# Two-layer trunk on one core: weight units made four ahead in five buffers, the norm's steps placed anew

## The chip, the core and the metric

One core of a Trainium2 chip runs the whole program, in one launch. Its engines have in-order instruction streams of their own: TensorE multiplies matrices (PE in the profile; its loads of stationary operands are PEld), VectorE (DVE) and ScalarE (ACT) work on tiles in SBUF and PSUM, SyncE (SP) issues the weight loads. PSUM has eight banks; TensorE writes nowhere else. The metric is the device time of one execution in microseconds (us).

## The reference

Two layers on 256 positions of width 1024, all in float32:

```
h += 0.5*SwiGLU(RMSNorm(h))                 (ffn1, width 2816)
u  = RMSNorm(h); one input projection of u feeds
     sparse attention (top-k keys), causal pooling, Mamba-2 SSD, three gates
h += W_out( sum_b sigmoid(gate_b) * Lift_b(branch_b) )
h += 0.5*SwiGLU(RMSNorm(h))                 (ffn2)
h += sigmoid(RMSNorm(h) W_g) * (p[i] W_p)   (ple)
```

and a last RMSNorm. RMSNorm divides a position by the root of the mean of its squares. The SSD branch has an RMSNorm of its own, over its 1024 channels, ahead of its lift. The gain of a norm is applied to the channels before a matmul; the factor r of a position can be multiplied in behind the matmul, since it belongs to a column of the result. The kernel uses that nearly everywhere.

## The kernel before

**Units.** All weights are cut into units of 128 x 1024 float32 (512 KB), 229 a layer, numbered here in the order in which they are used: 0 to 65 for ffn1, 66 to 69 for the narrow part of the input projection (704 columns each), 70 to 128 for the rest of the projection, the key-value matrices and the pooling, 129 to 144 for the lift, 145 to 152 for the output, then ffn2 and, from 219, ple; the second layer starts with unit 229. A unit is loaded by SP into a buffer `raw` (L135), rounded by ScalarE to `whi` (L136), and VectorE writes the remainder `wlo = raw - whi` (L137). A product then takes three matmuls (`mm3`, L159 to L161): uh x whi, ul x whi, uh x wlo, where uh and ul are the same two halves of the activations. A full unit feeds 24 matmuls of 128 x 128 by 256 columns.

**Ahead.** `unit()` makes the unit that is asked for and the next AHEAD = 3; `raw`, `whi` and `wlo` have four buffers each. So the cast and the remainder of unit n wait until TensorE has read unit n-4, and its load until VectorE has read the raw of n-4.

**Order.** Each engine's order of work is written by a scheduler that runs when the program is built: it goes by the code's order, by priorities, and by its own clock model of when operands will be there. Only TensorE's matmuls and transposes keep the program's order among those that pass `self.mm` and `self.transpose`. At run time the order of an engine is fixed; an instruction at its head that waits holds all behind it.

**The norm (`rnorm`).** The squares are added up in `acc` while h is written. Then: two matmuls by a column of ones (L106) sum over the channels; VectorE makes 1/sqrt by three Newton steps of two columns (`rsqrt`, L188 to L202); it writes two diagonal matrices dh and dl (L246, L247); two matmuls with a matrix of ones (`onesr`, L106; called the broadcast matmuls here) spread them to `pr`, in one of four `aux` banks; ScalarE copies `pr` to `r` (L255). `later()` runs the next piece of it, so it stands between the matmuls of the next stage. The results of that stage wait in four `mm` banks until r is there.

**Mix.** Its narrow projection (66 to 69) goes to two `aux` banks, then units 70 to 73 give the indexer's queries; VectorE takes their first bank pair by L437, writes u = h * gain * r by L446, and ScalarE and VectorE split u into uh and ul (L175, L176). From unit 74 on the matmuls read this u. The SSD's decay rates go through DRAM: written at L813, fetched back in broadcast by SP into three buffers `ab` (L820, L823), scanned on VectorE (L879).

**Lift.** For each of eight channel groups c, one unit multiplies attention and pooling into bank p1, another the SSD into p2. VectorE frees p1 by L593, and p2 by L597 and L598: t2 = (g3 + 1) * rs, t2 = t2 * p2, where rs is the r of the SSD's norm, whose matmuls stand among the lift's own.

Of the kernel before, what the change touches and what calls it, by code (L numbers as in the profile page):

```python
# [9 lines left out]
F = mybir.dt.float32  # L10
FR = mybir.dt.float32r
I32 = mybir.dt.int32
AF = mybir.ActivationFunctionType
OP = mybir.AluOpType
AX = mybir.AxisListType

P = 128
D = 1024
S = 256
# [4 lines left out]
EPS = 1e-6  # L24
NEG = -3.0e38
UNIT = 1024
# [38 lines left out]
class Builder:  # L65
# [43 lines left out]
        self.tc.keep_in_program_order(self.nc.tensor.transpose(*args))  # L109


    AHEAD = 3

    def unit(self, *key):
        self.used.append(key)
# [3 lines left out]
        assert self.order[i] == key  # L119
        for j in range(len(self.made), min(i + self.AHEAD, len(self.order) - 1) + 1):  # L120
            self.made.append(self.load(*self.order[j]))
        return self.made[i]

    def parts(self):
        raw = self.wp.tile([P, UNIT], F, tag="raw", name=self.name("raw"), bufs=4)
        hi = self.wp.tile([P, UNIT], FR, tag="whi", name=self.name("whi"), bufs=4)
        if self.gap is None:
            self.gap = self.wp.tile([P, LINE // 4], F, name="gap")
        lo = self.wp.tile([P, UNIT], FR, tag="wlo", name=self.name("wlo"), bufs=4)
        return raw, hi, lo  # L130

    def load(self, layer, u, n):
# [86 lines left out]
    def rnorm(self, late=False, gap=1):  # L219

        nc = self.nc
        r = self.t([P, S], tag="rs_r", bufs=3)
        v = self.t([P, 2], tag="rs_v", bufs=2)
        rc = self.t([P, 8], tag="rs_y", bufs=2)
        acc = None if late else self.acc

        def steps():
            nonlocal acc  # L230
            if late:
                for c in range(KD):
                    self.square(c, self.h[:, c])
                    if c % 4 == 3:
                        yield
                acc = self.acc
            ps = self.bank("aux")
            for h in range(2):
                self.mm(ps[:, h:h + 1], acc[:, h * P:(h + 1) * P], self.ones[:, :1],
                                 start=True, stop=True)  # L240
            nc.vector.tensor_scalar(v, ps[:, :2], 1.0 / D, EPS, op0=OP.mult, op1=OP.add)
            self.rsqrt(rc, v, 2)
            dh, dl = (self.t([P, 2, P], FR, tag="t1") for _ in range(2))
            for h in range(2):
                x = rc[:, h:h + 1]
                nc.vector.tensor_scalar(dh[:, h], self.ident, x, None, op0=OP.mult)  # L246
                nc.vector.scalar_tensor_tensor(dl[:, h], self.ident, x, dh[:, h].bitcast(F),  # L247
                                               op0=OP.mult, op1=OP.subtract)
            for _ in range(gap):
                yield  # L250
            pr = self.bank("aux")
            for i, d in enumerate((dh, dl)):
                self.mm(pr[:, :S], self.onesr, d.rearrange("p a b -> p (a b)"),
                                 start=(i == 0), stop=(i == 1))
            nc.scalar.copy(r, pr[:, :S])  # L255

        self.todo = steps()
        return rc, r

# [131 lines left out]

    def mix(self, layer, nxt):
        nc = self.nc
        rc, r = self.rnorm()
        rb = r[:, None, :].to_broadcast([P, 2, S])
        u0 = self.uh, self.ul

# [3 lines left out]
        big1 = self.a([P, KF, S], F, "gh")  # L401
        big2 = self.a([P, KF, S], F, "gl")
        ga = big1[:, :16].rearrange("p (a b) s -> p a b s", a=2)
        bc, cn = big1[:, 16:20], big1[:, 20:22]
        g3, zs = big2[:, :8], big2[:, 8:16]
        cb = big2[:, 16:19].rearrange("p a (b c) -> p a b c", b=2)
        idx = big2[:, 19:21]
        sm = self.a([P, 2, 96], F, "sm")[:, :, :88]
        ki2 = self.a([P, 2, 2, 64], F, "ki2")
        ss = self.t([P, 4], tag="ss", bufs=1)  # L410
        pb = []
        for h in range(2):
            ts = slice(h * P, (h + 1) * P)
            ps = self.bank("aux")
            for k in range(KD):
                w = wu[k // 2]
                s = slice((k % 2) * BF, (k % 2) * BF + 344)
                self.mm3(ps[:, :344], (u0[0][:, k, ts], u0[1][:, k, ts]),
                         (w[0][:, s], w[1][:, s]), k == 0, k == KD - 1)
            self.later()  # L420
            pb.append(ps)
        for h, ps in enumerate(pb):
            nc.scalar.mul(cn[:, h], ps[:, :256], rc[:, h:h + 1])
# [9 lines left out]
        for i in range(0, 4, 2):  # L433
            ps = self.in_pair(layer, T_QI + i, u0)
            self.later()
            t = self.t([P, 2, S])
# [7 lines left out]
        for k in range(KD):  # L444
            t = self.t([P, S], tag="t1")
            nc.vector.scalar_tensor_tensor(t, self.h[:, k], self.col(layer, "mix_norm", k), r,  # L446
                                           op0=OP.mult, op1=OP.mult)
# [4 lines left out]
        xs = self.a([P, 8, S], F, "uh", 2)  # L452
        q = [self.a([P, 4, S], FR, "a4", 7) for _ in range(2)]
# [77 lines left out]
        res = {}  # L531
# [25 lines left out]
            yield from self.attention(mb, q, kt, vt, ya)  # L557

        def states():
            res["ssd"] = yield from self.ssd(layer, sm, xs, bc, cb, zs)  # L560

        def pools():
            wpl = self.unit(layer, U_POOL, 512)
# [7 lines left out]
        with self.tc.issue_after(self.last.ins):  # L571
            self.weave((states(), 56), (attend(), 34), (pools(), 24), (gate, 43), apart=(0, 1))
        ysh, ysl, rs = res["ssd"]

        mh = self.a([P, 8, S], FR, "uh", 2)
        ml = self.a([P, 8, S], FR, "ul", 2)
        for c in range(8):
            p1, p2 = self.bank(), self.bank()
            w = self.unit(layer, U_LIFT + 2 * c, 1024)
            for b, y in enumerate((ya, yp)):  # L580
                for k in range(4):
                    s = slice((b * 4 + k) * P, (b * 4 + k + 1) * P)
                    self.mm3(p1[:, b * S:(b + 1) * S], (w[0][:, s], w[1][:, s]),
                             (y[:, 0, k], y[:, 1, k]), k == 0, k == 3)
            self.later()
            w = self.unit(layer, U_LIFT + 2 * c + 1, 1024)
            for k in range(8):
                s = slice(k * P, (k + 1) * P)
                self.mm3(p2[:, :S], (w[0][:, s], w[1][:, s]),
                         (ysh[k // 4][:, k % 4], ysl[k // 4][:, k % 4]), k == 0, k == 7)  # L590
            self.later()
            t = self.t([P, 2, S])
            nc.vector.scalar_tensor_tensor(t, ga[:, :, c], 1.0,  # L593
                                           p1.rearrange("p (a b) -> p a b", a=2),
                                           op0=OP.add, op1=OP.mult)
            t2 = self.t([P, S], tag="t1")
            nc.vector.scalar_tensor_tensor(t2, g3[:, c], 1.0, rs, op0=OP.add, op1=OP.mult)  # L597
            nc.vector.tensor_tensor(t2, t2, p2[:, :S], op=OP.mult)  # L598
            nc.vector.tensor_tensor(t[:, 0], t[:, 0], t[:, 1], op=OP.add)
            nc.vector.tensor_tensor(t2, t[:, 0], t2, op=OP.add)  # L600
            self.split(mh[:, c], ml[:, c], t2)
        self.new_u()
        for cs in ((0, 1), *((c,) for c in range(2, 8))):
            ps = [self.bank()[:, :S] for _ in cs]
# [167 lines left out]
        yield lambda: out(1)  # L772
        done(1)

    def ssd(self, layer, sm, xs, bc, cb, zs):
        nc = self.nc


        x = self.t([P, 2, 16], tag="dt_x", bufs=1)
# [16 lines left out]
        for k in (15, 13, 11, 9, 7, 5, 3):  # L796
# [5 lines left out]
                                       op0=OP.mult, op1=OP.mult)  # L802
        yield

        ps = self.bank("aux")
# [7 lines left out]
        nc.sync.dma_start(dram, rows)  # L813
        yield

        def fetch(g, h, q):
            x = self.t([P, 4, P], tag="ab", bufs=3)
            if q < 2:
                k = h * 16 + g * 8 + q * 4
                nc.sync.dma_start(x, dram[None, k:k + 4, :].to_broadcast([P, 4, P]))  # L820
            else:
                for i in range(2):
                    nc.sync.dma_start(x[i * 64:(i + 1) * 64],  # L823
                                      dram[None, 16 + g * 8 + i:16 + g * 8 + 8:2, :]
                                      .to_broadcast([64, 4, P]))
            return x

        wanted = [(g, h, q) for g in range(2) for h, q in ((0, 0), (0, 1), (1, 0), (1, 1), (1, 2))]
        rates = {}

        def rate(*key):
            i = wanted.index(key)
            for k in wanted[i:i + 3]:
                if k not in rates:
                    rates[k] = fetch(*k)
            return rates[key]


        for i, (a, b) in enumerate(((0, 0), (1, 1), (0, 1))):
            ps = self.bank("aux")  # L840
# [3 lines left out]
            v = ps[:, :S].rearrange("p (a b) -> p a b", a=2)  # L844
# [8 lines left out]
        for h in range(2):  # L853
            for g in range(2):
                ps = self.bank("aux")
# [12 lines left out]
        ps = self.bank("aux")  # L868
# [3 lines left out]
        for g in range(2):  # L872
            gs = slice(g * 4, (g + 1) * 4)
            for h in range(2):
                ms = self.a([P, 2, 4, P], F, "ct")
                for q in range(2):
# [9 lines left out]
                                            op=OP.mult)  # L886
                    yield
                ps = self.bank("aux")

                def near():  # L890
                    for j in range(8):
# [15 lines left out]
                                    op=OP.mult)  # L907
            po = self.bank("aux")
            e1 = self.t([P, 4, P])
            x = rate(g, 1, 2)  # L910
# [5 lines left out]
            for j in range(4):  # L916
                a = x0[:, 2 * j:2 * j + 2].rearrange("p a b -> p (a b)")
# [10 lines left out]
            for i in range(4):  # L928
                k = g * 4 + i
# [2 lines left out]
                self.split_scaled(ysh[g][:, i], ysl[g][:, i], y[:, k],  # L932
                                  self.col(layer, "ssd_norm", k))
                yield
        _, rs = self.rnorm()
        return ysh, ysl, rs

    def pool_group(self, layer, g, ps, wpl, yp):
# [242 lines left out]
```

## Time and profile before

| | |
|---|---|
| three runs | 1340.24, 1342.32, 1345.29 us; median 1342.32 |
| the profiled execution | 1341.97 us, of which 1340.1 are the span of its records |
| busy in that span | TensorE 98%, VectorE 78%, ScalarE 55% |
| DMA | 248.24 MB, mean 185 GB/s |
| TensorE's granted clock | 9 of 10 or more in all 40 slices |

How to read it: the span is cut into what each engine did and what it waited for. TensorE's matmuls are pipelined: one of 256 columns takes about 0.28 us from its start to its end, but in a steady row the next one starts 0.113 us later. So what TensorE loses at one place is read from the starts: the distance between two of them, less that pace. The waits that the profile names are a little shorter, since they count only from the end of the matmul before.

### The profile page before, as it was taken

What the parts mean: (1) busy time and instruction counts of PE and PEld (TensorE: products, weight loads), DVE (VectorE), ACT (ScalarE), POOL (GpSimd) and SP (SyncE); (2) the same over time, 40 slices, a digit from 0 to 9 for tenths busy, and PEclk for the clock granted to TensorE, in tenths of its full rate; (3) what the DMA queues carried; (4) which work ended last, traced back from release to release, by engine and by line L of the source; (5) the groups of instructions that cost most, each with busy time, mean ns of one, the idle gap of its engine ahead of it and who ended that gap; (6) DMA issues with size and microseconds to landing.
All of it is one profiled execution on the core that took longest, in us unless ns stands there. A gap on an engine that the chain in (4) does not pass through costs nothing.

```text
span 1340.1 us, 28299 instructions
## 1 busy us (share of the span) xinstructions
PE 1312.0 (98%) x11502; PEld 1297.7 (97%) x11502; DVE 1040.5 (78%) x1971; ACT 740.4 (55%) x1209; POOL 5.3 (0%) x17
## 2 busy tenths in 40 slices
PE   7999999999999999999999999999999999999997
PEld 7999999999999999999999999999999999999997
DVE  7877668987989777766887766779789888777666
ACT  5554446656864555544654454556477645555454
POOL 0000000000000000000000000000000000000000
PEclk9999999999999999999999999999999999999999
DMA  7666656576646666666556666546655556666661
GB/s 257 191 192 198 192 158 201 158 208 192 189 128 199 191 200 191 194 197 191 187 162 200 192 191 197 188 135 196 195 190 163 175 180 204 190 191 195 197 190 63
DMA packets 72385, 248.24 MB, mean 185 GB/s; under 512 B 7936, under 2 KB 10304, under 8 KB 72256
## 3 DMA queue, kind: packets, MB, share of 16 engines
q1 hardware_dynamic: 71392, 245.17, 59.5%
q8 instruction: 90, 1.47, 0.5%
q10 hardware_dynamic: 864, 1.28, 0.3%
q14 instruction: 39, 0.32, 0.1%
HBM read 245.33 MB, written 1.08 MB: 184 GB/s over the span
## 4 chain that ended last, share of the span: by engine, by line
PE 94%; DVE 3%; ACT 1%; issue 0%; DMA 0%; SPq 0%; DVEq 0%; ACTq 0%
PE mm L159 29%; PE mm L160 29%; PE mm L161 29%; PE aux L106 3%; PE aux L159 1%; PE aux L160 1%; PE aux L161 1%; DVE wlo L137 1%; PE aux L109 1%; ACT whi L136 0%; DMA h<-in_x_dram 0%; DVE t L446 0%; DVE t L993 0%; ACT t L213 0%; DVE ct L879 0%
## 5 line engine op out<-in xcount | busy, mean ns | idle before, releaser
L136 ACT CAST whi<-raw 128x1024 fp32r<-128x1024 f32 (+1 forms) x457 | 475.0, 1045 | 491.1 <-issue 245.2
L159 PE MATMUL mm<-uh,whi 128*128 128x256 f32 x2560 | 708.3, 278 | 12.6 <-ACT whi L153 6.7
L137 DVE TENSOR_TENSOR wlo<-raw,whi 128x1024 fp32r<-128x1024 f32 (+1 forms) x457 | 553.5, 1214 | 212.8 <-ACT whi L136 209.6
L160 PE MATMUL mm<-ul,whi 128*128 128x256 f32 x2560 | 709.0, 278 | 0.9 <-DVE ul L176 0.9
L161 PE MATMUL mm<-uh,wlo 128*128 128x256 f32 x2560 | 707.5, 278 | 2.0 <-DVE wlo L137 1.9
L159 PEld LDWEIGHTS mm<-uh,whi 128*128 128x128 f32 x2560 | 480.5, 188 | 15.9 <-ACT whi L153 6.7
L161 PEld LDWEIGHTS mm<-uh,wlo 128*128 128x128 f32 x2560 | 481.3, 188 | 3.2 <-DVE wlo L137 2.6
L160 PEld LDWEIGHTS mm<-ul,whi 128*128 128x128 f32 x2560 | 482.1, 188 | 2.3 <-DVE ul L176 1.3
L161 PE MATMUL mm<-gh,wlo 128*128 128x256 f32 x704 | 194.1, 276 | 0.0
L160 PE MATMUL mm<-gl,whi 128*128 128x256 f32 x704 | 194.1, 276 | 0.0
L159 PE MATMUL mm<-gh,whi 128*128 128x256 f32 x704 | 193.7, 276 | 0.0
L160 PEld LDWEIGHTS mm<-gl,whi 128*128 128x128 f32 x704 | 132.2, 188 | 0.0
L161 PEld LDWEIGHTS mm<-gh,wlo 128*128 128x128 f32 x704 | 132.2, 188 | 0.0
L159 PEld LDWEIGHTS mm<-gh,whi 128*128 128x128 f32 x704 | 131.9, 188 | 0.0
L159 PE MATMUL mm<-a,whi 128*128 128x256 f32 x256 | 69.8, 278 | 3.2 <-DVE t L593 1.3
L160 PE MATMUL mm<-a,whi 128*128 128x256 f32 x256 | 70.4, 277 | 0.0
L161 PE MATMUL mm<-a,wlo 128*128 128x256 f32 x256 | 70.3, 276 | 0.0
L159 PEld LDWEIGHTS mm<-a,whi 128*128 128x128 f32 x256 | 47.4, 188 | 4.0 <-issue 3.9
L160 PEld LDWEIGHTS mm<-a,whi 128*128 128x128 f32 x256 | 48.1, 188 | 0.0
L161 PEld LDWEIGHTS mm<-a,wlo 128*128 128x128 f32 x256 | 48.1, 188 | 0.0
L352 DVE TENSOR_TENSOR t<-mm,rs_r 128x256 f32<-128x256 f32 x88 | 37.3, 423 | 11.2 <-ACT rs_r L255 1.4
L357 DVE SCALAR_TENSOR_TENSOR t<-t,t 128x256 f32<-128x256 f32 x88 | 37.4, 425 | 3.1
(211 smaller groups left out, 1096.8 us busy)
## 6 DMA issues: line engine op xcount, KB each, us to landing
raw<-in_w_dram SPq DMA_DIRECT2D x447, 512.0 KB, 3.6
ab<-rates SPq DMA_DIRECT2D x16, 256.0 KB, 4.1
raw<-in_w_dram SPq DMA_DIRECT2D x8, 352.0 KB, 3.0
raw<-in_w_dram SPq DMA_DIRECT2D x4, 256.0 KB, 4.7
ab<-rates SPq DMA_DIRECT2D x8, 128.0 KB, 3.3
h<-in_x_dram SPq DMA_DIRECT2D x2, 256.0 KB, 4.2
h<-in_x_dram SPq DMA_DIRECT2D x1, 512.0 KB, 6.1
t<-in_p_dram ACTq DMA_DIRECT2D x2, 256.0 KB, 5.0
```

What stands on the lines that cost most here:

```text
L106: self.tc.keep_in_program_order(self.nc.tensor.matmul(*args, **kw))
L109: self.tc.keep_in_program_order(self.nc.tensor.transpose(*args))
L136: nc.scalar.copy(hi[:, :n], raw[:, :n])
L137: nc.vector.tensor_tensor(lo[:, :n], raw[:, :n], hi[:, :n].bitcast(F), op=OP.subtract)
L159: mm(ps, a[0], b[0], start=start, stop=False)
L160: mm(ps, a[0], b[1], start=False, stop=False)
L161: mm(ps, a[1], b[0], start=False, stop=stop)
L352: nc.vector.tensor_tensor(t, p1[0], r, op=OP.mult)
L357: nc.vector.scalar_tensor_tensor(g, th, 1.0, t, op0=OP.add, op1=OP.mult)
```

## The change

`AHEAD` is 4, and `whi` and `wlo` have five buffers; `raw` still has four. The rates are fetched into six rows of the tile `big1` that the gates will use later (`room`) and no longer into `ab`, and the small tile ki2 comes from the pool t1. In the lift, p2 is multiplied by the gate (g3 + 1) first, without rs, so both banks of a group can be freed before rs is known; groups that have no rs yet stand in the list `waiting`, and the product by rs is made for all of them once the norm has run through. In `rnorm`, the short steps and the copy to r stand under `high_priority(offset=160)`. The norms of mix and of the SSD have `gap=2` for 1, and in the narrow projection `later()` is called after every fourth block and not once at its end. No instruction is added or taken away; each engine has as many as before.

```diff
-    AHEAD = 3
+    AHEAD = 4
...
-        hi = self.wp.tile([P, UNIT], FR, tag="whi", name=self.name("whi"), bufs=4)
+        hi = self.wp.tile([P, UNIT], FR, tag="whi", name=self.name("whi"), bufs=5)
...
-        lo = self.wp.tile([P, UNIT], FR, tag="wlo", name=self.name("wlo"), bufs=4)
+        lo = self.wp.tile([P, UNIT], FR, tag="wlo", name=self.name("wlo"), bufs=5)
...
-        r = self.t([P, S], tag="rs_r", bufs=3)
+        r = self.t([P, S], tag="rs_r", bufs=2)
...
+            with self.tc.high_priority(offset=160):
+                ps = self.bank("aux")
...
+            with self.tc.high_priority(offset=160):
+                nc.scalar.copy(r, pr[:, :S])
...
-        rc, r = self.rnorm()
+        rc, r = self.rnorm(gap=2)
...
-        ki2 = self.a([P, 2, 2, 64], F, "ki2")
+        ki2 = self.t([P, 2, 2, 64], tag="t1")
...
-            self.later()
+                if k % 4 == 3:
+                    self.later()
...
+        waiting = []
...
-            nc.vector.scalar_tensor_tensor(t2, g3[:, c], 1.0, rs, op0=OP.add, op1=OP.mult)
-            nc.vector.tensor_tensor(t2, t2, p2[:, :S], op=OP.mult)
+            nc.vector.scalar_tensor_tensor(t2, g3[:, c], 1.0, p2[:, :S], op0=OP.add, op1=OP.mult)
             nc.vector.tensor_tensor(t[:, 0], t[:, 0], t[:, 1], op=OP.add)
-            nc.vector.tensor_tensor(t2, t[:, 0], t2, op=OP.add)
-            self.split(mh[:, c], ml[:, c], t2)
+            waiting.append((c, t, t2))
+            if self.todo is None:
+                for c1, t, t2 in waiting:
+                    nc.vector.tensor_tensor(t2, t2, rs, op=OP.mult)
+                    nc.vector.tensor_tensor(t2, t[:, 0], t2, op=OP.add)
+                    self.split(mh[:, c1], ml[:, c1], t2)
+                waiting = []
...
-            x = self.t([P, 4, P], tag="ab", bufs=3)
+            i = wanted.index((g, h, q)) % 3 * 2
+            x = room[:, i:i + 2].rearrange("p a (b c) -> p (a b) c", b=2)
...
-        _, rs = self.rnorm()
+        _, rs = self.rnorm(gap=2)
```

How the order moves, at the places that the prediction speaks of. First VectorE at the start of mix in layer 0, before; wlo_2628 and wlo_2663 are the remainders of units 74 and 75, rk is the norm of the indexer's keys, and L437 is the first instruction that reads r (rs_r):

```order
L137 TENSOR_TENSOR wlo_2628<-raw_2626,whi_2627 128x1024
L191 TENSOR_SCALAR rk_2768<-rs_t_2770 128x4
L195 TENSOR_TENSOR rs_t_2770<-rk_2768,rs_h_2769 128x4
L196 TENSOR_TENSOR rs_t_2770<-rs_t_2770,rk_2768 128x4
L137 TENSOR_TENSOR wlo_2663<-raw_2661,whi_2662 128x1024
L202 SCALAR_TENSOR_TENSOR rk_2768<-rs_t_2770,rk_2768 128x4
L437 TENSOR_TENSOR t_386_2656<-mm_2595,rs_r_2471 128x512
L446 SCALAR_TENSOR_TENSOR t_397_2727<-h,cc_93,rs_r_2471 128x256
```

The same place now; wlo_2634, wlo_2669 and wlo_2699 are units 75, 76 and 77, and L440 is the old L437:

```order
L137 TENSOR_TENSOR wlo_2634<-raw_2632,whi_2633 128x1024
L191 TENSOR_SCALAR rk_2774<-rs_t_2776 128x4
L137 TENSOR_TENSOR wlo_2669<-raw_2667,whi_2668 128x1024
L195 TENSOR_TENSOR rs_t_2776<-rk_2774,rs_h_2775 128x4
L137 TENSOR_TENSOR wlo_2699<-raw_2697,whi_2698 128x1024
L196 TENSOR_TENSOR rs_t_2776<-rs_t_2776,rk_2774 128x4
L440 TENSOR_TENSOR t_389_2662<-mm_2601,rs_r_2477 128x512
L449 SCALAR_TENSOR_TENSOR t_400_2733<-h,cc_93,rs_r_2477 128x256
```

The last remainder ahead of the first use of r was unit 75's and is now unit 77's. On ScalarE it is the same: before, the casts of units 74 and 75 stood ahead of the copy to r,

```order
L136 CAST whi_2627<-raw_2626 128x1024
L136 CAST whi_2662<-raw_2661 128x1024
L255 COPY rs_r_2471<-aux_2577 128x256
L136 CAST whi_2692<-raw_2691 128x1024
L175 CAST a_377_2593<-t_386_2656 128x512
```

and now those of 75, 76 and 77 do, with 78 right behind it:

```order
L136 CAST whi_2633<-raw_2632 128x1024
L136 CAST whi_2668<-raw_2667 128x1024
L136 CAST whi_2698<-raw_2697 128x1024
L257 COPY rs_r_2477<-aux_2571 128x256
L136 CAST whi_2795<-raw_2794 128x1024
L175 CAST a_380_2599<-t_389_2662 128x512
```

TensorE around the second broadcast matmul of that norm, now; whi_2493 and wlo_2494 are unit 72, whose buffers unit 77 takes next, and whi_2499 is unit 73:

```order
L160 MATMUL mm_2666<-ul_1745,whi_2493 128x256
L161 MATMUL mm_2666<-uh_1744,wlo_2494 128x256
L159 MATMUL mm_2666<-uh_1744,whi_2499 128x256
L160 MATMUL mm_2666<-ul_1745,whi_2499 128x256
L161 MATMUL mm_2666<-uh_1744,wlo_2500 128x256
L159 MATMUL mm_2666<-uh_1744,whi_2499 128x256
L106 MATMUL aux_2571<-t_373_2541,onesr 128x256
L160 MATMUL mm_2666<-ul_1745,whi_2499 128x256
```

It stands 17 matmuls later than before, as all matmuls of this norm do (17 of unit 70 now come ahead of its first one): 20 matmuls of unit 73 are left behind it for 37 before, and unit 72 is read through only four matmuls ahead of it. Last, VectorE in the norm at the start of ffn1 in layer 1, before, from the Newton steps to L352, the first use of r; wlo_9053 and wlo_9111 are units 237 and 238:

```order
L200 SCALAR_TENSOR_TENSOR rs_t_8936<-rs_y_8866,rs_h_8935 128x1 x2
L202 SCALAR_TENSOR_TENSOR rs_y_8866<-rs_t_8936,rs_y_8866 128x2
L137 TENSOR_TENSOR wlo_9053<-raw_9051,whi_9052 128x1024
L200 SCALAR_TENSOR_TENSOR rs_t_8936<-rs_y_8866,rs_h_8935 128x1 x2
L202 SCALAR_TENSOR_TENSOR rs_y_8866<-rs_t_8936,rs_y_8866 128x2
L246 TENSOR_SCALAR t_1316_8949<-ident,rs_y_8866 128x128 x2
L247 SCALAR_TENSOR_TENSOR t_1317_8950<-ident,rs_y_8866,t_1316_8949 128x128 x2
L137 TENSOR_TENSOR wlo_9111<-raw_9109,whi_9110 128x1024
L352 TENSOR_TENSOR t_1333_9081<-mm_8869,rs_r_8864 128x256
```

and now, where wlo_9049 and wlo_9107 are units 238 and 239:

```order
L137 TENSOR_TENSOR wlo_9049<-raw_9047,whi_9048 128x1024
L202 SCALAR_TENSOR_TENSOR rs_y_8862<-rs_t_8932,rs_y_8862 128x2
L137 TENSOR_TENSOR wlo_9107<-raw_9105,whi_9106 128x1024
L200 SCALAR_TENSOR_TENSOR rs_t_8932<-rs_y_8862,rs_h_8931 128x1 x2
L202 SCALAR_TENSOR_TENSOR rs_y_8862<-rs_t_8932,rs_y_8862 128x2
L200 SCALAR_TENSOR_TENSOR rs_t_8932<-rs_y_8862,rs_h_8931 128x1 x2
L202 SCALAR_TENSOR_TENSOR rs_y_8862<-rs_t_8932,rs_y_8862 128x2
L247 TENSOR_SCALAR t_1309_8945<-ident,rs_y_8862 128x128 x2
L248 SCALAR_TENSOR_TENSOR t_1310_8946<-ident,rs_y_8862,t_1309_8945 128x128 x2
L354 TENSOR_TENSOR t_1326_9077<-mm_8865,rs_r_8860 128x256
```

Two of the three Newton rounds and both diagonals now stand behind the remainder of unit 239, which takes the buffer of unit 234; the matmuls of unit 234 are the last ahead of the broadcast matmuls there, before and now.

## Rows read from the trace of the kernel before

**Rows 1.** The page's first part: busy us (share of the span) xinstructions.

```profile
PE 1312.0 (98%) x11502; PEld 1297.7 (97%) x11502; DVE 1040.5 (78%) x1971; ACT 740.4 (55%) x1209; POOL 5.3 (0%) x17
```

**Rows 2.** TensorE's waits: what waited for whom, us in total, times, longest.

```profile
PE mm L159 <- ACT whi L153: 6.7, 1, 6.7
PE mm L159 <- ACT whi L136: 4.2, 5, 1.1
...
PE mm L161 <- DVE wlo L137: 1.9, 2, 0.9
```

**Rows 3.** Windows of 20 us: length, busy us (x instructions) of each engine, clock, DMA.

```profile
180.00:200.00 20.00, 20.00 (x160) 20.00 (x159) 12.73 (x31) 8.72 (x13) 0.00 (x0) 1.00 0.48 144
200.00:220.00 20.00, 18.48 (x159) 18.08 (x159) 19.15 (x50) 11.49 (x28) 0.00 (x0) 1.00 0.66 211
...
860.00:880.00 20.00, 18.48 (x145) 18.09 (x144) 19.15 (x50) 11.56 (x29) 0.00 (x0) 0.91 0.67 211
```

**Rows 4.** Timeline of TensorE, start of mix: start, us, instruction, [idle before <-releaser].

```profile
206.45 0.28 PE L106 MATMUL aux<-t,onesr 128*128 128x256 f32 x1
...
210.78 0.39 PE L159 MATMUL mm<-uh,whi 128*128 128x256 f32 x2
212.25 0.39 PE L159 MATMUL mm<-uh,whi 128*128 128x256 f32 x1 [1.08 <-ACT whi L136]
213.08 0.39 PE L160 MATMUL mm<-ul,whi 128*128 128x256 f32 x1 [0.44 <-DVE ul L176]
```

**Rows 5.** Timeline of ScalarE at the same place.

```profile
205.52 1.05 ACT L136 CAST whi<-raw 128x1024 fp32r<-128x1024 f32 x1 [1.24 <-PE mm L160]
206.76 0.37 ACT L255 COPY rs_r<-aux 128x256 f32<-128x256 f32 x1 [0.19 <-PE aux L106]
```

**Rows 6.** Timeline of VectorE at the same place.

```profile
201.97 1.22 DVE L137 TENSOR_TENSOR wlo<-raw,whi 128x1024 fp32r<-128x1024 f32 x1
...
205.86 0.16 DVE L196 TENSOR_TENSOR rs_t<-rs_t,rk 128x4 f32<-128x4 f32 x1
206.61 1.23 DVE L137 TENSOR_TENSOR wlo<-raw,whi 128x1024 fp32r<-128x1024 f32 x1 [0.59 <-PE mm L160]
207.75 0.16 DVE L202 SCALAR_TENSOR_TENSOR rk<-rs_t,rk 128x4 f32<-128x4 f32 x1
207.82 0.68 DVE L437 TENSOR_TENSOR t<-mm,rs_r 128x512 f32<-128x512 f32 x1
...
212.61 1.08 DVE L176 TENSOR_TENSOR ul<-t,uh 128x256 fp32r<-128x256 f32 x3
```

**Rows 7.** The page's part on DMA issues: KB each, median us to landing.

```profile
raw<-in_w_dram SPq DMA_DIRECT2D x447, 512.0 KB, 3.6
```

**Rows 8.** Timelines of ScalarE, TensorE and SP while attention and SSD alternate.

```profile
313.09 1.05 ACT L136 CAST whi<-raw 128x1024 fp32r<-128x1024 f32 x1 [2.39 <-PE aux L161]
...
317.19 0.39 PE L161 MATMUL mm<-uh,wlo 128*128 128x256 f32 x1 [0.94 <-DVE wlo L137]
...
303.56 1.28 SPq L820 DMA_DIRECT2D ab<-rates  x3
```

**Rows 9.** Timeline of TensorE in the lift.

```profile
410.10 0.36 PE L159 MATMUL mm<-a,whi 128*128 128x256 f32 x1 [0.64 <-DVE t L593]
...
414.04 0.36 PE L159 MATMUL mm<-a,whi 128*128 128x256 f32 x1 [0.94 <-DVE t L598]
```

**Rows 10.** Timelines of TensorE and VectorE, start of ffn1 in layer 1.

```profile
675.47 0.39 PE L159 MATMUL mm<-uh,whi 128*128 128x256 f32 x1 [0.39 <-ACT uh L179]
...
686.29 0.82 PE L106 MATMUL aux<-t,onesr 128*128 128x256 f32 x2 [0.63 <-DVE t L246]
688.28 0.38 PE L159 MATMUL mm<-uh,whi 128*128 128x256 f32 x1 [1.17 <-DVE t L352]
...
685.09 0.34 DVE L200 SCALAR_TENSOR_TENSOR rs_t<-rs_y,rs_h 128x1 f32<-128x1 f32 x2
...
687.80 0.42 DVE L352 TENSOR_TENSOR t<-mm,rs_r 128x256 f32<-128x256 f32 x1
```

More of the change, by code (lines that the diff above doesn't have):

```diff
@@ L236, in steps @@
                 acc = self.acc
[L237 to L248, printed above, removed]
+            with self.tc.high_priority(offset=160):
+                ps = self.bank("aux")
+                for h in range(2):
+                    self.mm(ps[:, h:h + 1], acc[:, h * P:(h + 1) * P], self.ones[:, :1],
+                                     start=True, stop=True)
+                nc.vector.tensor_scalar(v, ps[:, :2], 1.0 / D, EPS, op0=OP.mult, op1=OP.add)
+                self.rsqrt(rc, v, 2)
+                dh, dl = (self.t([P, 2, P], FR, tag="t1") for _ in range(2))
+                for h in range(2):
+                    x = rc[:, h:h + 1]
+                    nc.vector.tensor_scalar(dh[:, h], self.ident, x, None, op0=OP.mult)
+                    nc.vector.scalar_tensor_tensor(dl[:, h], self.ident, x, dh[:, h].bitcast(F),
+                                                   op0=OP.mult, op1=OP.subtract)
             for _ in range(gap):
@@ L254, in steps @@
                                  start=(i == 0), stop=(i == 1))
-            nc.scalar.copy(r, pr[:, :S])
+            with self.tc.high_priority(offset=160):
+                nc.scalar.copy(r, pr[:, :S])
         self.todo = steps()
@@ L559, in states @@
         def states():
-            res["ssd"] = yield from self.ssd(layer, sm, xs, bc, cb, zs)
+            res["ssd"] = yield from self.ssd(layer, sm, xs, bc, cb, zs, big1[:, 16:22])
         def pools():
@@ L773, in attention, with ssd @@
         done(1)
-    def ssd(self, layer, sm, xs, bc, cb, zs):
+    def ssd(self, layer, sm, xs, bc, cb, zs, room):
         nc = self.nc
@@ L814, in ssd @@
         yield
+        wanted = [(g, h, q) for g in range(2) for h, q in ((0, 0), (0, 1), (1, 0), (1, 1), (1, 2))]
         def fetch(g, h, q):
-            x = self.t([P, 4, P], tag="ab", bufs=3)
+            i = wanted.index((g, h, q)) % 3 * 2
+            x = room[:, i:i + 2].rearrange("p a (b c) -> p (a b) c", b=2)
             if q < 2:
@@ L826, in fetch @@
             return x
-        wanted = [(g, h, q) for g in range(2) for h, q in ((0, 0), (0, 1), (1, 0), (1, 1), (1, 2))]
         rates = {}
```

## Prediction

> **What bounds the kernel now.** I read the busy shares first. TensorE is busy for 1312.0 of 1340.1 us [rows 1], so 28 us of idle time is all that a change of order can win, and whatever VectorE (1040.5) and ScalarE (740.4) save is worth nothing by itself. Then the waits by cause [rows 2]: 6.7 us are the first cast of the kernel, while the first weights arrive; the rest comes in waits of about 1 us. Then windows of 20 us [rows 3]: most read 20.00 as from 180 to 200, and a few read 18.1 to 19.5. The stretch from 200 to 220 lost 1.52, and its twin in layer 1 lost the same to 0.01, so each place of mix counts twice. Last the timelines of those stretches, for what stands in front of what.
>
> The pace comes from [rows 4]: from the broadcast matmul at 206.45 to the first matmul that reads the new u at 210.78 are 38 steps (37 matmuls stand between, by the order), 4.33 us, 0.114 each. A recorded wait is shorter than the loss: at 212.25 the start is 1.47 behind a pair that takes two steps, a loss of 1.24 for 1.08 recorded, so I add 0.16 to recorded waits. Losses that the change can touch: 1.24 + 0.72 = 1.96 at the start of mix [rows 4] (at 213.08 the loss is 0.83 less a step), 0.94 + 0.16 = 1.10 where attention and SSD alternate [rows 8], 0.64 + 0.94 + 2 x 0.16 = 1.90 in the lift [rows 9], all these in both layers; once, at the start of ffn1 in layer 1, 0.39 + 0.16 = 0.55 for the last u and 0.63 + 1.17, with 0.75 more from pipeline refills around them, 2.55 [rows 10]. In all 2 x 4.96 + 3.10 = 13.0 us, 1.0% of the time.
>
> **Start of mix.** Before: the copy to r starts 0.31 us after the second broadcast matmul (206.45 to 206.76) [rows 4, 5]; VectorE, with the remainder of unit 75 from 206.61, reaches L437 at 207.82 and the first ul at 212.61 [rows 6]; TensorE goes on at 213.08, 0.47 behind that. Now all matmuls of this norm stand 17 steps later: 17 x 0.114 = 1.93, so the second broadcast is at 208.38. Ahead of the copy stands the cast of unit 77, which needs the buffer of unit 72. TensorE reads that one's whi for the last time six steps ahead of the broadcast, at 207.70, and lets go 0.28 later, at 207.98. The cast also needs its raw tile: that load is issued when the remainder of unit 73 is done, 201.97 + 1.22 = 203.2 [rows 6] and about the same now, since that remainder follows the narrow projection's buffers; with the median 3.6 us of a load [rows 7] it lands at 206.8, and were loads to queue up, later. So the cast runs from 208.0 to 209.05 (1.05 us [rows 5]), the copy follows and is done by 209.4, the remainder of unit 77 takes 1.2 more, and L440 starts near 210.3. That is 2.5 us later than 207.82. From there to the first ul the order has the same instructions and one more product of two banks (0.68 by L437, 0.6 without its overlap): 210.3 + 4.79 + 0.6 = 215.7, and TensorE goes on at 216.2 for 213.08. **+3.1 us, per layer**; if the load lands as late as the cast would like it no longer, +0.4, so +3.5. I take the middle, +3.3, twice: +6.6. Nothing covers it: unit 73 has only 20 matmuls left behind the broadcast, 2.3 us, where it was 4.2. The third unit's cast, which TensorE waited for at 212.25, is early now, but it is paid for in front of the copy.
>
> That rests on engines that don't pass a waiting instruction. The trace shows it: at 205.86 VectorE finishes L196, the operand of L202, which takes 0.16 us and yet starts at 207.75, behind a remainder that waited 0.59 us for TensorE [rows 6]. The Trainium skill says the same (TensorE: Matmul & The Clock Gate, "Architectural detail"): ScalarE's and VectorE's queues are strict FIFO. If they were not, the copy would start at 208.7, and the place would cost some 2 us less in each layer, a sum below zero.
>
> **Attention and SSD alternating.** The cast at 313.09 waited 2.39 us for TensorE, and at 317.19 TensorE waited for the remainder made from it [rows 8]. Unit 110 waited for unit 107, which TensorE reads here; with five buffers it takes that of 105, read several us earlier, and cast and remainder (1.05 + 1.21) come ahead of the scans. The 1.10 goes: **-1.1 per layer, -2.2.** The rates now land in rows that other work reads until about 304.4; their loads were issued at 303.56 in a row of three [rows 8] and wait for that on SP, with the next unit's load in front or behind. They take about 4 us and the scans start at 313, so there are some 4 us of cover; if it went, the price is the delay less that, nothing on one side and 1 us a layer on the other. I take 0.
>
> **Lift.** TensorE waited for L593 and L598 [rows 9]: banks p2 of the first groups were held until rs was there, while p1 stood behind remainders. Now p2 is freed by one product without rs, and only SBUF tiles wait for the norm. VectorE's instructions are as many, and the dh and dl for the broadcast are ready 2 us before TensorE gets there. **-1.9 per layer, -3.8**; between 0, if the product by rs at VectorE's head blocks the next banks, and -3.8. I take the whole, since four banks rotate with about 2 us to spare each.
>
> **ffn2, ple, output.** The order of TensorE is the same there to a row; the norm's losses stay. 0, between -1.5 and +1.5 for the high priority of the short steps.
>
> **Start of ffn1 in layer 1.** Sixteen matmuls of unit 233 now fill the wait for the last u: -0.55. But the remainder of unit 239 stands ahead of two Newton rounds and both diagonals, and it needs the buffer of unit 234, which TensorE reads until the very broadcast that waits for these diagonals. That matmul would come, without its waits, at 686.29 - 0.63 - 0.55 = 685.1. Then the cast, 1.05, the remainder, 1.14 to the next start: 687.4 at the earliest, 688.3 if raw 239 lands late. From the last round to the first use of r were 687.80 - 685.09 = 2.7 us [rows 10], now plus a round (0.6): L354 at 690.7 to 691.6, TensorE 0.48 later, 691.2 to 692.1 for 688.28. **+2.9 to +3.8 with the 0.55 already in it; I take +3.0.** The start of layer 0's ffn1 has no wait to lose or win. 0.
>
> **Sum.** 6.6 - 2.2 - 3.8 + 3.0 = +3.6 us. The profiled execution took 1341.97, which is 0.35 below the median of the runs, 1342.32. So 1345.6 us, +0.3% and inside the 0.5% (6.7 us) that a measurement can tell from no change.
>
> **Rivals.** *A, faster.* The deeper buffering and the preferred short steps work as a whole: the copy and the diagonals pass the splits in time, and the two new waits stay as long as the old ones. Then -2.2 - 3.8 - 0.55 = -6.5, 1335.4; with all losses gone 1329.0. For it: five buffers give each split a whole unit, 2.7 us, more of slack. Against it: the order above, in which at both places the split of a unit whose buffer is freed last stands in front. The Trainium skill speaks for it (Perfetto Trace Analysis, "Identifying Performance Opportunities"): a gap that repeats on the engine that should be full can mean too few buffers; here that fits the wait at 317.19 and not those on the norm. *B, slower.* Raw tiles still have four buffers, and the load of a unit is issued by the remainder four units back; if units 77 and 239 land 1 us or more behind TensorE's release at the three places, each such us goes straight through the cast, the copy and L440 into TensorE's wait. With landing 5 to 6 us after the issue, 208.2 to 209.2 in mix and as late in ffn1, that is up to 1.2 at each, and with the lift's gain halved: 3.6 + 3.6 + 1.9 = +9.1, 1351.1. It decides from about +1 us of landing. Against it: the median of 3.6, and TensorE's idle time lets loads catch up. *C, nothing moves.* The norm's waits end where they did, since they hang on TensorE's own place and on the Newton steps, and the lift's banks wait as before: 1341 to 1343. For it: only 13 us were there. Against it: the 17 steps in the order.
>
> **Chances.** The forecast with its neighbours (a net of +1 to +6), 0.45; C, 0.15; A, 0.16, three quarters of it beyond -0.5%; B, 0.24. So faster 0.14, within 0.5% 0.60, slower 0.26. The range: 1335.4 of A is cut at its upper edge, the forecast's bounds (mix +-0.4, ffn1 +0.8, lift +3.8, ffn2 and ple +-1.5) give 1342 to 1352, B's middle 1351 and the 2 us by which runs differ are let in: 1336.0 to 1353.0. The forecast's own range is 1342 to 1349.
>
> **What would show it.** In the changed profile: TensorE's wait for ul or uh at the start of mix near 5 us in place of 2, with the cast of unit 77 ahead of the copy to r and a wait for TensorE before it; the window from 200 to 220 at about 15.5 busy; no wait on wlo near 316 and none on L597 or L601 in the lift; one wait of 5 to 6 us at 686. Wrong if the copy at mix starts before 208.9, if the lift waits on, or if the wait in ffn1 is under 3 us: then the remainder didn't stand behind TensorE's release.

## The result, and the profile after

The changed kernel takes 1352.43 us (median of five runs, 1349.97 to 1355.65) for 1343.9 before (five runs, the three of the table above and two more, 1340.24 to 1345.29): a ratio of 1.0069, 95% interval 1.0047 to 1.0091. So it is 0.7% slower, where I had forecast 0.3% and put most of the chances within 0.5%; the interval begins just under that bound. The median lies inside the range, 0.6 us under its upper end, which rival B had set and not the forecast's sum.

The profiled execution has a span of 1351.0 us for 1340.1. TensorE's waits, by what it waited for (us in total, times, longest; before: [rows 2]):

```profile
PE mm L160 <- DVE ul L176: 6.7, 2, 3.5
PE mm L159 <- ACT whi L153: 6.3, 1, 6.3
PE aux L106 <- DVE t L247: 5.8, 1, 5.8
PE mm L159 <- ACT uh L175: 3.9, 2, 2.1
PE mm L159 <- DVE t L354: 1.9, 3, 0.9
...
PE mm L159 <- ACT whi L136: 0.2, 1, 0.2
```

The waits on a remainder (L137) and on the lift's products are gone. Three new ones have come: for uh and ul at the start of mix, in both layers, and for the diagonals at the start of ffn1 in layer 1. TensorE at the start of mix, layer 0, from the second broadcast matmul on (before: [rows 4]):

```profile
210.31 0.28 PE L106 MATMUL aux<-t,onesr 128*128 128x256 f32 x1
...
214.97 0.62 PE L159 MATMUL mm<-uh,whi 128*128 128x256 f32 x3 [2.10 <-ACT uh L175]
219.13 0.58 PE L160 MATMUL mm<-ul,whi 128*128 128x256 f32 x1 [3.54 <-DVE ul L176]
```

From the start just before each, less the pace, that is 2.26 + 3.71 = 5.97 us where it was 1.96, and in layer 1 5.35 for 1.95. ScalarE in front of it, the casts of units 76 and 77 and the copy to r (before: [rows 5]):

```profile
208.60 1.06 ACT L136 CAST whi<-raw 128x1024 fp32r<-128x1024 f32 x1 [0.43 <-DMA raw<-in_w_dram]
210.98 1.05 ACT L136 CAST whi<-raw 128x1024 fp32r<-128x1024 f32 x1 [1.32 <-DVE wlo L137]
211.93 0.37 ACT L257 COPY rs_r<-aux 128x256 f32<-128x256 f32 x1
```

and VectorE, the remainder of unit 77, the first product by r and the first ul (before: [rows 6]):

```profile
212.06 1.23 DVE L137 TENSOR_TENSOR wlo<-raw,whi 128x1024 fp32r<-128x1024 f32 x1 [1.07 <-ACT whi L136]
213.21 0.16 DVE L196 TENSOR_TENSOR rs_t<-rs_t,rk 128x4 f32<-128x4 f32 x1
213.28 0.69 DVE L440 TENSOR_TENSOR t<-mm,rs_r 128x512 f32<-128x512 f32 x1
...
218.66 1.09 DVE L176 TENSOR_TENSOR ul<-t,uh 128x256 fp32r<-128x256 f32 x3
```

The order does what was forecast: cast 77, then the copy, remainder 77, then L440. Three distances have grown: the second broadcast matmul stands 17 matmuls later, 1.9 us; from it to the first product by r are 2.97 us for 1.37 before (210.31 to 213.28; 206.45 to 207.82 [rows 4, 6]); and from that to the first ul 5.38 for 4.79. Together that is 4.1 us. The cast of unit 77 lies in the second of them. It came 1 us later than forecast against TensorE, since its load did: that was issued at 205.95 and took 4.9 us, to 210.9 (below, the one load issued between 205.8 and 206.2; columns: KB, us to landing).

```profile
raw<-in_w_dram SPq DMA_DIRECT2D x1, 512.0 KB, 4.9
```

The profile puts the cast's wait down to the remainder of unit 76, which ended at the same moment; the order gives that cast no operand from it. What had not been forecast at all stands in the windows of 2 us behind (length, busy us (x instructions) of PE, PEld, DVE, ACT, POOL, then TensorE's granted clock, the share of the DMA engines and GB/s):

```profile
214.00:216.00 2.00, 0.62 (x3) 0.41 (x3) 2.00 (x6) 2.00 (x6) 0.00 (x0) 1.00 0.84 281
216.00:218.00 2.00, 0.00 (x0) 0.00 (x0) 2.00 (x4) 1.39 (x3) 0.00 (x0) 0.50 0.12 47
...
220.00:222.00 2.00, 2.00 (x11) 2.00 (x11) 2.00 (x6) 0.14 (x1) 0.00 (x0) 0.50 0.45 176
222.00:224.00 2.00, 2.00 (x16) 2.00 (x15) 1.90 (x10) 0.66 (x2) 0.00 (x0) 0.80 0.00 0
224.00:226.00 2.00, 2.00 (x20) 2.00 (x19) 0.65 (x3) 0.37 (x1) 0.00 (x0) 1.00 0.00 0
```

TensorE idled, its clock fell to 0.50 (1.2 GHz), and when work came back it ran 11 matmuls in 2 us in place of 18 to 20 (starts 0.213 us apart for 0.113) until the clock rose. Its busy time is full there, and no wait is recorded. In ffn1 of layer 1 the same three things are seen: casts of units 238 and 239 that wait for their loads, the broadcast matmul behind them (before: [rows 10]), and a mean clock of 0.87 from 684 to 710.

```profile
687.97 1.05 ACT L136 CAST whi<-raw 128x1024 fp32r<-128x1024 f32 x1 [1.14 <-DMA raw<-in_w_dram]
690.55 1.04 ACT L136 CAST whi<-raw 128x1024 fp32r<-128x1024 f32 x1 [1.53 <-DMA raw<-in_w_dram]
...
694.55 1.01 PE L106 MATMUL aux<-t,onesr 128*128 128x256 f32 x2 [5.76 <-DVE t L247]
696.49 0.58 PE L159 MATMUL mm<-uh,whi 128*128 128x256 f32 x1 [0.92 <-DVE t L354]
```

The 10.9 us between the spans, from the distances between like matmuls in both traces: start of the kernel +1.9; waits at mix +4.0 and +3.4; in ffn1 of layer 1 5.1 more at the broadcast and 1.2 less at the last u, the pipeline's refills around it counted in; attention and SSD -2.2; lift -3.8; matmuls at half clock behind the waits at mix +1.7 and +0.7 (before had such a stretch of its own in layer 1) and behind that in ffn1 +1.9; all the rest -0.6. The start differs between profiles of one order (the last matmul of unit 73 starts at 212.6 here and at 210.4 in the second experiment, where nothing was changed ahead of it but room for buffers), so it is left out of the causes.

### The profile page after: what moved, and what is told of

Same layout as the page of the kernel before. It is cut to its first block, busy times and chain, and to the rows that moved or that the text cites. A ratio compares the mean times of both kernels' runs of the same rounds, so it can differ in the third digit from the quotient of the medians.

```text
span 1351.0 us, 28294 instructions
## 1 busy us (share of the span) xinstructions
PE 1316.8 (97%) x11502; PEld 1304.2 (97%) x11502; DVE 1041.8 (77%) x1971; ACT 742.8 (55%) x1209; POOL 3.4 (0%) x17
## 4 chain that ended last, share of the span: by engine, by line
PE 93%; DVE 2%; DMA 1%; issue 1%; ACT 1%; SPq 0%; DVEq 0%; ACTq 0%
PE mm L159 29%; PE mm L161 29%; PE mm L160 29%; PE aux L106 3%; DMA raw<-in_w_dram 1%; ACT whi L136 1%; DVE wlo L137 1%; PE aux L109 1%; PE aux L160 1%; PE aux L159 1%; PE aux L161 1%; DMA h<-in_x_dram 0%; DVE t L449 0%; DVE rs_t L200 0%; ACT uh L179 0%
## 5 line engine op out<-in xcount | busy, mean ns | idle before, releaser
L137 DVE TENSOR_TENSOR wlo<-raw,whi 128x1024 fp32r<-128x1024 f32 (+1 forms) x457 | 554.4, 1215 | 219.2 <-ACT whi L136 215.2
```

The lines of the kernel that those rows point to most:

```text
L137: nc.vector.tensor_tensor(lo[:, :n], raw[:, :n], hi[:, :n].bitcast(F), op=OP.subtract)
```

## Experiments

Without the priorities, or with the old gap and calls in mix, or with AHEAD = 3, the changed kernel has on every engine the same order, row for row. What acts are the buffers, the lift, and the rates' room, which frees the space that the buffers need. Each ratio below is against the kernel before on the same chip (median 1342.05 us in the first four, 1341.94 in the last two).

**e1: four buffers again.**

```diff
-        hi = ... tag="whi", ... bufs=5)
+        hi = ... tag="whi", ... bufs=4)
-        lo = ... tag="wlo", ... bufs=5)
+        lo = ... tag="wlo", ... bufs=4)
```

> The changed kernel with four buffers of whi and wlo for five; AHEAD 4, the rates' room, the lift, the norms' places and priorities stay. Theory 1 (the fifth buffer lets the scheduler put one more split ahead of the norm's steps, and TensorE waits for it): the order at the start of mix and of ffn1 in layer 1 is that of before again, so the losses there are 2.0 us (for 6.2 and 5.6 with five buffers) and about 3 (for 7.6), the clock stays up there but for what before shows, the 1.1 us at the alternation of attention and SSD come back, and the 3.8 us of the lift stay saved: about 4 us below before, some 12 below the changed kernel. Theory 2 (the later place of the norm's matmuls by gap=2 and the early calls, or the priorities, do it): the waits of 5 to 6 us stay and the time is that of the changed kernel or 2 us above it.

Measured: 1345.65 us, ratio 1.0024 (1.0010 to 1.0037). The mechanism is as theory 1 had it: at the start of mix the waits of before are back to 0.01 us, with the clock at 1.00,

```profile
212.29 0.38 PE L159 MATMUL mm<-uh,whi 128*128 128x256 f32 x1 [1.08 <-ACT whi L136]
213.11 0.39 PE L160 MATMUL mm<-ul,whi 128*128 128x256 f32 x1 [0.44 <-DVE ul L176]
```

and so is the 1.1 us at 316. Theory 2 falls as it was put: the priorities, the gap and the calls are all still there. What e1 does not part are the two things that the fifth buffer brings into the order at mix, the split of unit 77 ahead of the copy and the norm's matmuls 17 places later: with four buffers both are gone, and 37 matmuls stand behind the second broadcast again. The time does not follow (6.8 below the changed kernel where some 12 were expected), since a wait had come that I had not looked for in the order, at the start of ffn2 in both layers:

```profile
472.51 0.28 PE L106 MATMUL aux<-t,onesr 128*128 128x256 f32 x1
475.29 0.39 PE L159 MATMUL mm<-uh,whi 128*128 128x256 f32 x1 [2.50 <-DVE t L354]
```

2.66 us for 0.63 before: 4.1 in all, against 3.8 saved in the lift. It is the same picture as at mix: on ScalarE a cast that waits for TensorE (472.60) now stands ahead of the copy to r (473.55), and on VectorE a remainder (473.67) ahead of the first product by r (474.81). The losses thus sum to about those of before, and the profiled execution took 1342.57, the lowest of ten runs; the others go up to 1350.4, at granted clocks of 0.992 to 0.996 for 0.995 to 0.998 before.

**e2: five raw buffers as well.**

```diff
-        bufs = {"t2": 6, "t1": 6}.get(tag, 1) if bufs is None else bufs
+        bufs = {"t2": 4, "t1": 6}.get(tag, 1) if bufs is None else bufs
...
-        raw = ... tag="raw", ... bufs=4)
+        raw = ... tag="raw", ... bufs=5)
```

> The changed kernel with five raw buffers too (the pool t2 pays with four buffers for six). Theory L (the casts of units 77 and 239 wait for their loads, which wait for a free raw tile): loads are issued one unit earlier, the cast ahead of the copy to r starts 1 us or more earlier, the loss at the start of mix falls from 5.6 to 6.2 us to about 4, in ffn1 from 7.6 to 5 or 6; in all 4 to 6 us below the changed kernel, about 1 to 2 more if the clock then stays up at a place. Theory P (they wait for TensorE to let go of the weight buffer, as the prediction had it): the waits stay within 0.5 us and the time is that of the changed kernel.

Measured: 1348.57 us, ratio 1.0047 (1.0033 to 1.0062); 3.9 below the changed kernel (of the 5.0 between the profiled spans, 2.2 are the start). The cast of unit 77, and that of 239, now wait for TensorE and no longer for a load:

```profile
207.70 1.05 ACT L136 CAST whi<-raw 128x1024 fp32r<-128x1024 f32 x1 [0.81 <-PE mm L160]
208.65 0.36 ACT L257 COPY rs_r<-aux 128x256 f32<-128x256 f32 x1
...
686.22 1.04 ACT L136 CAST whi<-raw 128x1024 fp32r<-128x1024 f32 x1 [0.94 <-PE mm L160]
```

```profile
212.48 0.62 PE L159 MATMUL mm<-uh,whi 128*128 128x256 f32 x3 [1.85 <-ACT uh L175]
215.85 0.58 PE L160 MATMUL mm<-ul,whi 128*128 128x256 f32 x1 [2.75 <-DVE ul L176]
...
690.22 1.01 PE L106 MATMUL aux<-t,onesr 128*128 128x256 f32 x2 [3.92 <-DVE t L247]
```

The loss at mix is 4.93 us in each layer (2.01 + 2.92 less the pace), 3.0 more than before, and in ffn1 the broadcast's 5.8 are 3.2 more. So theory L holds for the part above the forecast (1.0, 0.4 and 1.8 us), and theory P for the rest. It is less than theory L had expected at mix, since TensorE's release is right behind. The clock still falls: its mean over the span is 0.990 in both kernels. Of the 3.0 us that are left at mix, 1.9 are the 17 matmuls, 0.6 the splits between the second broadcast (208.06) and L440 (210.00), and 0.6 the one product more.

**e3: the wait filled.**

```diff
             self.split(u[0][:, k], u[1][:, k], t)
+            if k == 0:
+                junk = self.bank("aux")
+                for _ in range(30):
+                    self.mm(junk[:, :S], self.onesr, u[0][:, k], start=True, stop=True)
```

> The changed kernel with 30 extra matmuls (of the first uh with the matrix of ones, into an aux bank that nothing reads) in the wait for the first ul, at the start of mix in both layers; 30 x 0.113 = 3.4 us, just shorter than that wait of 3.5 and 3.2 us. Theory C (the clock falls to half during the wait and the matmuls behind it pay about 1.7 us at each place): the granted clock stays at 1.00 there, the time falls by 3 to 4 us against the changed kernel, with VectorE's chain at the same times. If the clock costs nothing or falls anyhow in the first wait of 2.1 us: 0 to +1 us.

Measured: 1349.44 us, ratio 1.0053 (1.0037 to 1.0070): 60 matmuls more, and 3.0 us less than the changed kernel, as theory C had it. Place by place, from like matmuls in the two traces: 2.1 us less at mix in layer 0, 1.6 in layer 1, 0.3 in ffn1, and a start 1.2 later. VectorE's chain did not keep its times: the wait for ul ends 0.4 us earlier in layer 0 and 0.7 later in layer 1. What the clock gave back is therefore 1.7 and 2.3 us. TensorE and its clock at the place, the filling first:

```profile
215.90 3.69 PE L106 MATMUL aux<-uh,onesr 128*128 128x256 f32 x30 [1.85 <-ACT uh L175]
```

```profile
214.00:216.00 2.00, 0.15 (x2) 0.10 (x1) 2.00 (x7) 2.00 (x4) 0.00 (x0) 1.00 0.78 254
216.00:218.00 2.00, 2.00 (x18) 2.00 (x19) 2.00 (x6) 1.73 (x6) 0.00 (x0) 1.00 0.75 266
...
220.00:222.00 2.00, 2.00 (x18) 2.00 (x19) 2.00 (x7) 0.00 (x0) 0.00 (x0) 1.00 0.72 246
```

The clock stays at 1.00 although the first wait of 2 us is still there: without the second wait behind it, the first does not bring the clock down here.

**e4: five buffers of whi, four of wlo.**

```diff
-        lo = ... tag="wlo", ... bufs=5)
+        lo = ... tag="wlo", ... bufs=4)
```

> The changed kernel with five buffers of whi and four of wlo. The order puts units 73 to 75 ahead of the copy to r in mix and unit 76's remainder behind the first product by r; in ffn1 the remainder of 238 stands behind the diagonals. Theory 1: no split that waits stands ahead of the norm's steps, so the loss at mix is 2 to 2.5 us, at ffn1 2 to 3, the lift's 3.8 us stay saved: 4 to 6 us below before. Theory 2 (the later place of the norm's matmuls): the second broadcast matmul is 8 matmuls later than before, 0.9 us, so mix loses 1 us more per layer than before and the time is within 2 us of before's.

Measured: 1339.26 us, ratio 0.9983 (0.9968 to 0.9997). Theory 1's direction, and less than it expected: mix loses 3.1 us in each layer where 2 to 2.5 were expected and before lost 1.96. The copy to r, the first product by r, the first ul and TensorE's wait for it:

```profile
210.53 0.37 ACT L257 COPY rs_r<-aux 128x256 f32<-128x256 f32 x1
...
211.02 0.69 DVE L440 TENSOR_TENSOR t<-mm,rs_r 128x512 f32<-128x512 f32 x1
...
215.80 0.42 DVE L176 TENSOR_TENSOR ul<-t,uh 128x256 fp32r<-128x256 f32 x1
...
216.28 0.58 PE L160 MATMUL mm<-ul,whi 128*128 128x256 f32 x1 [2.94 <-DVE ul L176]
```

The clock falls behind it (0.93 from 210 to 235). From L440 to the first ul VectorE takes 4.78 us, as before (4.79 [rows 6]), with one remainder in between in both kernels. What is later is L440 itself: the second broadcast matmul (209.33) has 29 matmuls behind it for 37, which is 0.9 us, and L440 follows it by 1.69 us for 1.37. So at mix theory 2 had the size, 1 us more per layer. The waits at 316, in the lift and in ffn2 are all gone, and ffn1 keeps 2.9 at the broadcast (2.55 before).

**e5: the splits behind the chain.** e4 with AHEAD = 3 and the order fixed where a wait was left:

```diff
+        if self.order and len(self.made) in (77, 306, 237, 238):
+            self.tc.keep_in_program_order(x)          # x: the remainder, L137
...
         for k in range(KD):
-            self.split(u[0][:, k], u[1][:, k], t)
+            if k:
+                keep(x)                               # x: the product by r
+            nc.scalar.copy(u[0][:, k], t)
+            late.append((k, t))
+            if k:
+                low()                                 # ul of k - 1, kept in order too
+        low()
+        for i in range(0, 4, 2):                      # the queries' products, moved behind
+            t = self.t([P, 2, S])
+            keep(nc.vector.tensor_tensor(t, pq[i // 2], rb, op=OP.mult))
+            self.split(qi[0][:, i:i + 2], qi[1][:, i:i + 2], t)
```

> Five buffers of whi and four of wlo as in e4, AHEAD 3, and order by hand where a wait is left: at the start of mix each ul stands right behind the next product by r, the queries' products behind all of them, the remainder of unit 77 behind that; at the start of ffn1 in layer 1 the remainders of 237 and 238 behind what is traced before them. If the norm's chain on VectorE is what TensorE waits for: the loss at the start of mix falls from 3.4 to 1 to 1.5 us in each layer and the clock no longer falls there, in ffn1 from 3.9 to about 3; 4 to 6 us below e4, 7 to 9 below before. If something else holds TensorE there (the casts of unit 78, the banks, units 76 and 77 being late now), a new wait of that size shows behind it and the time is that of e4.

Measured: 1331.47 us (1329.65 to 1332.44), ratio 0.9920 (0.9907 to 0.9933). It beats both kernels, by 10.5 us the one before, where 7 to 9 were expected. The largest of TensorE's waits that are left:

```profile
PE mm L161 <- ACT whi L155: 6.5, 1, 6.5
PE mm L161 <- DVE t L356: 1.6, 1, 1.6
PE mm L162 <- DVE ul L452: 1.0, 4, 0.4
PE aux L106 <- ACT t L215: 0.8, 1, 0.8
```

Mix loses 0.96 and 0.72 us, no new wait stands behind it, and the clock reads 1.00 from 210 to 235, from 684 to 710 and from 870 to 900 (0.94 there before). In ffn1 2.3 us are left at the broadcast. Units 76 and 77 are split later and TensorE doesn't notice: VectorE's chain was what it waited for. The second broadcast matmul stands where it stands in e4; what has shrunk is the way from the first product by r to the first ul, 2.0 us for 4.8. How the gain divides is not shown: with five buffers of whi and four of wlo, AHEAD = 3 alone moves rows too (268 of VectorE's 1939).

**e6: the lift alone**, in the kernel before: the lift's part of the diff and nothing else.

> The kernel before with the lift's part of the change alone: p2 freed without rs, the product by rs made later. The waits in the lift (1.9 us per layer) go. In the order, the broadcast matmuls of ffn2's norm stand 15 and 4 matmuls later than before, as in e1. If the lift is what moved them: ffn2 loses 2.7 us per layer as in e1 for 0.6 before, and the two cancel: the time is that of before, +-2 us. If ffn2's loss in e1 came from another part (AHEAD, the priorities): ffn2 keeps its 0.6 and the time falls by 3.8 us.

Measured: 1345.36 us, ratio 1.0026 (1.0015 to 1.0036). The lift's waits are gone and ffn2 has e1's:

```profile
PE mm L159 <- DVE t L352: 6.2, 3, 2.5
```

(2.1 before in the same row's kind; the three are ffn2 twice and ffn1.) So it is the lift's new code that brings ffn2's wait, in a stage 60 us behind it: there the broadcast matmuls stand 15 and 4 places later, and the same cast and remainder as in e1 stand ahead of the copy and of the first product by r. The mean clock is 0.91 from 470 to 490 and from 1130 to 1150, for 1.00 before, which goes with a time above before's rather than equal.

## Why the prediction was wrong

- **Order at mix and ffn1: right.** The fifth buffer moves the order as forecast, and e1, which takes it away, brings the waits of before back. At mix that is two things at once: the norm's matmuls 17 places later (1.9 of the 4.1 us; forecast 1.93) and the split of unit 77 ahead of the copy and of L440 (1.6). No run moves the splits alone, so these shares come from distances in the traces. In ffn1 the broadcast matmuls have their old place, and the splits stand ahead of the diagonals. e5, with the chain put together again, shows that VectorE's chain is what TensorE waits for: the waits nearly go.
- **Size at mix, +3.3 a layer: it was +4.0 and +3.4.** The step that failed is "with the median 3.6 us of a load it lands at 206.8". The sign that I had named, a wait for TensorE before the cast of unit 77, did not come: it waited for its load. That load was issued 0.8 us later than I had put it (205.95, less the 1.9 by which this profile starts later, for 203.2), since the remainder of unit 73 now stands behind the norm's L247; and it took 4.9 us for 3.6. The trace of the kernel before had this to read: there the load of unit 77, issued at 203.2, took 5.2 us,

```profile
raw<-in_w_dram SPq DMA_DIRECT2D x1, 512.0 KB, 5.2
```

  and I took the median of all 447 loads [rows 7] in its place. With the load in time (e2) the place costs 3.0: the arithmetic from the rows was good to 0.3 us.
- **Size in ffn1, +3.0 net: it was +3.9** (696.49 for 688.28, less the 4.3 us by which the matmuls ahead of the place are late already). The same step: "688.3 if raw 239 lands late" was the bound I should have taken; that load was issued at 685.64, behind a remainder that had moved, and took 4.8 us. In e2, with the load in time, it is +2.1. So two errors cancel in part: the late load costs 1.8, and the matmuls that fill the wait for the last u gave back about 1.2 with the refills around it, where I had taken 0.55.
- **The clock: no term at all.** This is the larger miss. I priced a wait at its length. The three long waits brought the clock to 0.50, and TensorE paid 1.7 and 1.9 us more behind two of them and 0.7 more than before behind the third. e3 shows it as cause at mix: with the second wait filled the clock stays up, and 1.7 and 2.3 us come back. For ffn1 no run fills the wait. The hint was in my own rows: the window of layer 1 has a clock of 0.91 where layer 0 has 1.00 [rows 3], and I read only its busy time. The Trainium skill (TensorE: Matmul & The Clock Gate, "The HAM clock gate") says that idle time halves the clock and that there is no level between; the windows agree, 0.50 and 1.00 with mixtures only where it changed within a window.
- **Attention and SSD, lift, ffn2, rates: right.** -2.2, -3.8, 0 and 0 were forecast and measured (no wait of TensorE on the scans, L889, which read the rates, is left in the profile). That ffn2 stayed at 0.63 was luck in part: with four buffers the lift's code makes it 2.66 (e1, e6).
- **Sum.** +3.6 was forecast, the span grew by 10.9: 4.3 are the clock, 0.8 mix and 0.9 ffn1, 1.9 the start, and other places took 0.6 less. Rival B was nearest to what happened, in its mechanism (loads behind four raw buffers, late by 1.0, 0.4 and 1.8 us) and in its time, 1351.1, but it had 0.24 of the chances, and that its time fits is in part luck: it halved the lift's gain, which came whole, and knew nothing of the clock. C fell: the waits moved by 2 to 5 us. A's "as a whole" fell too, though its gain was to be had: e5 lies at 1331.47, between A's 1335.4 and 1329.0.

Left open: why the same wait keeps the clock in one place and not in the other (below), how much of e1's and e6's spread that explains run by run, and why loads take 5 us at these places.

## What to carry to other kernels

A deeper buffer is also a licence for the scheduler: here it moved work of the future ahead of the chain that the present waits for, so that a buffer that comes free last sat in front of the shortest step, and it moved the chain's own matmuls later. Look in the new order at what stands ahead of each short chain, and ask of each such row when its operand, its buffer and its load will be there, with the load's issue taken from the new order too, and its time from the loads at that place and not from the median of the run. Price a wait of TensorE together with what follows it, by the granted clock of the windows behind; and after a local gain look at the next stages, whose order may have moved as well.

## What the runs showed of the hardware that I had not expected

- The clock can fall for a wait that elsewhere leaves it alone. Before, the start of mix loses 1.96 us in layer 0 and 1.95 in layer 1, in the same order; in layer 0 the clock stays at 1.00, in layer 1 it reads

```profile
874.00:876.00 2.00, 2.00 (x14) 2.00 (x14) 2.00 (x5) 0.62 (x1) 0.00 (x0) 0.64 0.50 193
876.00:878.00 2.00, 2.00 (x11) 2.00 (x11) 2.00 (x7) 0.80 (x2) 0.00 (x0) 0.51 0.39 70
```

  The wait of 2.50 us at the start of ffn2 does the same: in e1 the clock reads 1.00 from 470 to 490, in e6 0.91.

- A stretch at half clock shows no wait: its price, 1.7 and 1.9 us behind two of the waits, lies in matmuls that take longer.
- A load of 512 KB took 3.6 us in the median of the run before. At the start of mix in layer 0, where one followed another by 1.1 to 2.4 us, loads took 3.6 to 5.2 us in the kernel before and 3.6 to 5.0 in the changed one.
